# Two gate products of a recurrent branch, split by heads into 64-row matmuls

## The chip, the cores and the metric

The kernel runs on one core of a Trainium2 chip. The metric is device time in microseconds, as the median of several runs of one program. TensorE is called PE here, VectorE DVE, ScalarE ACT, GpSimd POOL and SyncE SP, as the profile calls them.

## The reference

A block of an encoder for one sequence of 512 tokens and 1024 channels: RMS norm, one wide projection, three token mixers side by side (a gated convolution, a gated linear recurrence RG-LRU, and RWKV-7 time mixing), a gated merge, an output projection, and a squared-ReLU MLP. What the change touches are the two gate products of RG-LRU. There are 16 heads of 64 channels, and both gates multiply each head's `u` by a 64 x 64 matrix of that head:

```
xb = x.reshape(Bsz, S, LRU_HEADS, LRU_BW)
gate_a = sigmoid(einsum('bshi,hij->bshj', xb, w_a).reshape(Bsz, S, C) + b_a)
gate_i = sigmoid(einsum('bshi,hij->bshj', xb, w_i).reshape(Bsz, S, C) + b_i)
log_a = -LRU_C * gate_a * softplus(a_param)
a = exp(log_a)
u = x * gate_i * sqrt(-expm1(2.0 * log_a))
```

A linear recurrence over time with `a` and `u` follows.

## The kernel before

All tiles hold channels on the 128 partitions and the 512 tokens along the free axis. For accuracy each fp32 operand of a large product is split into a high and a low fp32r part, and a product is three matmuls (`mm3`, lines 166 to 168: high by high, high by low, low by high) that add up in one PSUM bank. A projection (`proj`, line 307) is 8 such triples, 24 matmuls of 128 x 128 weights by 512 tokens, out of `hh` and `hl`; its weights come by DMA into `raw`, are cast to `whi` on ACT (line 145) and subtracted to `wlo` on DVE (line 102), three buffers deep. Its bank is from pool `pp`.

The recurrent branch lies in `ab(q)`, q from 0 to 7, two heads of 64 channels each. Its gate products take `u` split into `uh` and `ul`, and the gate weights from `load_sw` with the tag `swb`. Each gate's weight is a 128 x 128 tile with two 64 x 64 blocks on the diagonal (two heads) and zeros elsewhere, one tile per gate:

```
swh, swl = load_sw(wk, "swb", q, 2, 2)
pga = pm.tile([P, S], F32, tag="pm", name="pga")
mm3(pga, swh[:, 0], swl[:, 0], uh, ul)
ga = W("u2")
ac.activation(ga, pga, AF.Tanh, bias=pv("ba", q), scale=0.5)
```

and the same once more for `pgi` and `gi` (lines 776 to 784). I call the six matmuls of one q a gate set, and count the sets from 1 to 8 (q = 0 to 7). The pool `pm`, from which both banks come, has two banks, and others use it too: in `amat` (line 517) the 16 products pA of a half of the chunks go to four banks, three of pool `pc` and one of `pm`; four multiplies by a mask on DVE (`AXt`, line 529) read and free them; then 16 transposes pB (line 548) go through four such banks and are copied out by ACT (line 549). The pA products are 64 rows deep, and turn by turn in the lower and the upper half of the rows.

The order of the work comes from a scheduler that places the instructions on each engine by its own estimate of their times. `weave` (line 831) lets a critical generator (`krv`, `amat`, `inverse`, `chain`) run at a raised priority and feeds it pieces of `ab` and later `gate` as filling. So the gate sets stand between other work: set 1 beside `amat` of group 0, set 2 beside group 1, set 4 beside group 2, sets 3, 5, 6 and 7 among projections, and set 8 within `chain`, the steps over 8 chunks of RWKV-7 (pu, py, pS: small matmuls of 64 columns). Each engine works through its instructions in the order given. ACT after a gate computes `a`, `ga` and a GELU (lines 787 to 798).

`gate(q)` (line 735) loads another 128 x 128 weight from the same array `sw` (index 4 of 5), and `pack` (line 1051) lays these arrays out on the host.

Of the kernel before, what the change touches and what calls it, by code (L numbers as in the profile page):

```python
# [9 lines left out]
F32 = mybir.dt.float32  # L10
# [8 lines left out]
P = 128  # L19
# [77 lines left out]
def block_kernel(ctx, tc, xt, win, par, mulr, sw, wout, w1, w2, fg, cst, eyes, out):  # L97
# [67 lines left out]
    def mm3(ps, wh, wl, xh, xl, start=True, stop=True):  # L165
        pe.matmul(ps, wh, xh, start=start, stop=False)  # L166
        pe.matmul(ps, wh, xl, start=False, stop=False)  # L167
        pe.matmul(ps, wl, xh, start=False, stop=stop)  # L168
# [566 lines left out]
    def gate(q):  # L735

        yc = wk.tile([P, S], F32, tag="g3", name="yc")
        gp.dma_start(yc, mpd[q])
        gt = wk.tile([P, S], F32, tag="gc", name="gc")
        t = yield from proj(("gc", q))  # L740
        ac.activation(gt, t, AF.Tanh, bias=pv("mgc", q), scale=0.5)
        swh, swl = load_sw(wk, "swc", q, 4, 1)
        pg = pm.tile([P, S], F32, tag="pm", name="pg2")
        mm3(pg, swh[:, 0], swl[:, 0], lgh, lgl)
        stt(gt, gt, 1.0, pg, ADD, MUL)
        GQ[q] = gq_tile(q)
        ac.activation(GQ[q], gt, AF.Copy, scale=dvp(HLG, q))
        stt(gt, BV[q], pv("lb", q), gt, ADD, MUL)
        stt(BV[q], gt, 0.5, yc, MUL, ADD)
        yield  # L750

    def ab(q):
# [20 lines left out]
        t = yield from proj(("c", q))  # L773
        ac.copy(cs, t)
        yield
        swh, swl = load_sw(wk, "swb", q, 2, 2)
        pga = pm.tile([P, S], F32, tag="pm", name="pga")
        mm3(pga, swh[:, 0], swl[:, 0], uh, ul)
        ga = W("u2")
        ac.activation(ga, pga, AF.Tanh, bias=pv("ba", q), scale=0.5)  # L780
        pgi = pm.tile([P, S], F32, tag="pm", name="pgi")
        mm3(pgi, swh[:, 1], swl[:, 1], uh, ul)
        gi = W("u3")
        ac.activation(gi, pgi, AF.Tanh, bias=pv("bi", q), scale=0.5)
        stt(u, gi, 1.0, u, ADD, MUL)
        a = W("u4")
        ac.activation(a, ga, AF.Exp, scale=dvp(N4, q), bias=dvp(N4, q))
# [263 lines left out]
def pack(inp):  # L1051
    g = {k: np.ascontiguousarray(np.asarray(a)) for k, a in inp.items()}
    z = {}
    z["xt"] = g["x"].reshape(S, D).T.reshape(KT, P, S)
    win = g["w_in"][0]
    cols = np.concatenate(COLS)
    z["win"] = win[:, cols].reshape(KT, P, len(COLS), P).transpose(2, 1, 0, 3).reshape(len(COLS), P, 1024)
    nat = lambda a: a.reshape(KT, P).T
    per = lambda a: a[PERM].reshape(KT, P).T
    mu = g["rwkv_mu"][0]  # L1060
    vecs = {"mu_k": mu[1024:2048], "mu_r": mu[0:1024], "kk": g["rwkv_kk"][0], "ka": g["rwkv_ka"][0],
            "w0": g["rwkv_w0"][0], "a0": g["rwkv_a0"][0], "rk": g["rwkv_rk"][0].reshape(-1),
            "mu_v": mu[2048:3072], "ap": g["lru_a_param"][0], "lcb": g["lru_conv_b"][0],
            "ba": g["lru_ba"][0], "bi": g["lru_bi"][0], "lg": g["rwkv_lnx_g"][0],
            "lb": g["rwkv_lnx_b"][0], "mga": g["merge_b"][0][0:1024],
            "mgb": g["merge_b"][0][1024:2048], "mgc": g["merge_b"][0][2048:3072],
            "n1": g["norm1_g"][0], "n2": g["norm2_g"][0]}
    for i in range(3):
        vecs[f"ca{i}"] = g["conv_a_w"][0, i]
    for i in range(4):  # L1070
        vecs[f"lc{i}"] = g["lru_conv_w"][0, i]
    z["par"] = np.stack([(per if n in PAR_Q else nat)(vecs[n]) for n in PAR], axis=1)
    z["mulr"] = mu[3072:3328].reshape(2, P).T
    sw = np.zeros((8, P, 5, P), np.float32)
    g2 = g["rwkv_g2"][0][:, PERM]
    for j in range(8):
        js = slice(j * P, (j + 1) * P)
        sw[j, 0:64, 0] = g["rwkv_w2"][0][:, js]
        sw[j, 64:128, 0] = g["rwkv_w2"][0][:, js]
        sw[j, 0:64, 1] = g["rwkv_a2"][0][:, js]  # L1080
        sw[j, 64:128, 1] = g["rwkv_a2"][0][:, js]
        sw[j, :, 4] = g2[:, js]
        for jj in range(2):
            hd = PERM[j * P + 64 * jj] // 64
            r = slice(64 * jj, 64 * jj + 64)
            sw[j, r, 2, r] = g["lru_wa"][0, hd]
            sw[j, r, 3, r] = g["lru_wi"][0, hd]
    z["sw"] = sw
    z["wout"] = g["w_out"][0][PERM].reshape(KT, P, KT, P).transpose(2, 1, 0, 3).reshape(KT, P, 1024)
    z["w1"] = g["mlp_w1"][0].reshape(KT, P, NF, P).transpose(2, 1, 0, 3).reshape(NF, P, 1024)  # L1090
    z["w2"] = g["mlp_w2"][0].reshape(NF, P, 1024)
    z["fg"] = g["final_g"].reshape(1, D)
    cst = np.zeros((P, 3, P), np.float32)
    idx = np.arange(P)
    cst[:, 0] = np.eye(P)
    cst[:, 1] = (idx[:, None] // 64) == (idx[None] // 64)
    s_, t_ = idx[:, None] % 64, idx[None] % 64
    cst[:, 2] = np.where(idx[None] < 64, s_ < t_, s_ <= t_)
    z["cst"] = cst.reshape(P, 3 * P)
    z["eyes"] = np.tile(np.eye(32, dtype=np.float32).reshape(1, 1024), (P, 1))  # L1100
    return {k: np.ascontiguousarray(a, dtype=a.dtype) for k, a in z.items()}
# [21 lines left out]
```

## Time and profile before

| | |
|---|---|
| median of 3 runs | 1045.11 us (1043.26 to 1046.57) |
| the profiled execution, its own time | 1047.99 us |
| its span, first to last instruction | 1045.8 us |
| mean granted TensorE clock | 0.994 |
| busy: PE / DVE / ACT / POOL | 1023.8 / 647.1 / 479.7 / 111.0 us |
| the gate activations (lines 780 and 784), 16 in all | 5.6 + 5.6 us |

How to read it: the profile is one execution, taken instruction by instruction; 2.2 us of its own time lie outside the span. An engine's busy time is the time in which at least one of its instructions ran. A record of a matmul is longer than the distance to the next one, since a matmul's end overlaps the beginning of the next; so what a matmul costs in a stream is read from the starts. The timeline merges neighbours of the same line into one row with their count. An fp32 matmul of pA, pu or py leaves two records, an fp32r one (projections, gates) leaves one.

### The profile page before, as it was taken

The page shows a single profiled execution, that of the slowest core. Times are in us where ns is not written, and L with a number is a line of the kernel's source. Part 1 is how long each engine was busy: PE and PEld are TensorE (multiplying, and loading weights), DVE is VectorE, ACT ScalarE, POOL GpSimd, SP SyncE. Part 2 cuts the span into 40 slices and gives each one's busy share as a digit, 9 for nine tenths or more (in the row PEclk, how much of TensorE's full clock was granted, in tenths as well). Part 3 has the DMA queues.
Part 4 walks back from the last instruction along what each step waited for, and adds up shares of the span by engine and source line. Part 5 has one row for each costly group of instructions (what it writes and reads, how often), then busy time and mean ns, then how long its engine had stood idle before and what let it go on. Part 6 is the DMA issues. An engine that isn't in the chain of part 4 may idle for free.

```text
span 1045.8 us, 15536 instructions
## 1 busy us (share of the span) xinstructions
PE 1023.8 (98%) x6204; PEld 833.4 (80%) x6204; DVE 647.1 (62%) x1086; ACT 479.7 (46%) x694; POOL 111.0 (11%) x181
## 2 busy tenths in 40 slices
PE   8999999999999999999999999999999999999996
PEld 5777877888878788888788878878888888888885
DVE  6997597599865875995567787554444442222224
ACT  7756453655545636455454444343434332221124
POOL 1013011201112112012122101010000000000001
PEclk8999999999999999999999999999999999999998
DMA  7344644734446346333987424443233335333322
GB/s 227 118 128 117 176 131 128 209 111 134 121 136 176 117 140 202 113 119 115 315 263 223 160 89 153 140 161 96 89 98 101 101 99 186 98 101 101 98 84 81
DMA packets 44504, 145.23 MB, mean 139 GB/s; under 512 B 6096, under 2 KB 9680, under 8 KB 43408
## 3 DMA queue, kind: packets, MB, share of 16 engines
q1 hardware_dynamic: 29472, 91.02, 27.5%
q0 software_dynamic: 14240, 52.18, 17.3%
q8 instruction: 48, 0.79, 0.3%
q10 hardware_dynamic: 720, 1.05, 0.3%
q14 instruction: 24, 0.20, 0.1%
HBM read 117.49 MB, written 26.74 MB: 138 GB/s over the span
## 4 chain that ended last, share of the span: by engine, by line
PE 86%; DVE 10%; issue 2%; ACT 1%; DMA 1%; SPq 0%; DVEq 0%; ACTq 0%
PE pp L166 13%; PE pp L167 13%; PE pp L168 13%; PE acc L166 7%; PE acc L167 7%; PE acc L168 7%; PE p L167 5%; PE p L166 5%; PE p L168 5%; DVE wlo L102 2%; PE py L662 1%; PE pu L652 1%; PE pu L672 1%; DVE rk L105 1%; PE pB L548 1%
## 5 line engine op out<-in xcount | busy, mean ns | idle before, releaser
L102 DVE TENSOR_TENSOR wlo<-raw,whi 128x1024 fp32r<-128x1024 f32 (+1 forms) x164 | 198.0, 1208 | 262.7 <-ACT whi L145 262.7
L145 ACT CAST whi<-raw 128x1024 fp32r<-128x1024 f32 (+1 forms) x164 | 169.9, 1036 | 323.1 <-PE acc L168 125.0
L166 PE MATMUL pp<-hh,whi 128*128 128x512 f32 x688 | 271.0, 394 | 0.4 <-DVE rs L105 0.4
L167 PE MATMUL pp<-hl,whi 128*128 128x512 f32 x688 | 270.1, 393 | 0.0
L168 PE MATMUL pp<-hh,wlo 128*128 128x512 f32 x688 | 269.1, 391 | 0.2 <-DVE wlo L102 0.2
L166 PEld LDWEIGHTS pp<-hh,whi 128*128 128x128 f32 x688 | 129.1, 188 | 28.6 <-DVE rs L105 0.9
L168 PEld LDWEIGHTS pp<-hh,wlo 128*128 128x128 f32 x688 | 129.2, 188 | 27.6 <-DVE wlo L102 0.6
L167 PEld LDWEIGHTS pp<-hl,whi 128*128 128x128 f32 x688 | 129.2, 188 | 26.4
L166 PE MATMUL p<-h2h,whi 128*128 128x512 f32 (+1 forms) x264 | 101.4, 384 | 0.0
L167 PE MATMUL p<-h2l,whi 128*128 128x512 f32 (+1 forms) x264 | 101.2, 383 | 0.0
L168 PE MATMUL p<-h2h,wlo 128*128 128x512 f32 (+1 forms) x264 | 101.1, 383 | 0.0
L166 PE MATMUL acc<-whi,ah 128*128 128x512 f32 x256 | 99.6, 389 | 0.0
L167 PE MATMUL acc<-wlo,ah 128*128 128x512 f32 x256 | 99.6, 389 | 0.0
L168 PE MATMUL acc<-whi,al 128*128 128x512 f32 x256 | 99.6, 389 | 0.0
L168 PEld LDWEIGHTS p<-h2h,wlo 128*128 128x128 f32 x264 | 49.6, 188 | 9.7
L166 PEld LDWEIGHTS p<-h2h,whi 128*128 128x128 f32 x264 | 49.6, 188 | 9.7
L167 PEld LDWEIGHTS p<-h2l,whi 128*128 128x128 f32 x264 | 49.7, 188 | 9.5
L168 PEld LDWEIGHTS acc<-whi,al 128*128 128x128 f32 x256 | 48.0, 188 | 10.1
L166 PEld LDWEIGHTS acc<-whi,ah 128*128 128x128 f32 x256 | 48.0, 188 | 9.9
L167 PEld LDWEIGHTS acc<-wlo,ah 128*128 128x128 f32 x256 | 48.0, 188 | 9.9
L992 ACT CAST ah<-r 128x512 fp32r<-128x512 f32 x32 | 19.9, 622 | 43.4 <-DVE r L102 43.4
L102 DVE TENSOR_TENSOR al<-r,ah 128x512 fp32r<-128x512 f32 x32 | 22.2, 692 | 21.5 <-ACT ah L992 21.4
(308 smaller groups left out, 1344.9 us busy)
## 6 DMA issues: line engine op xcount, KB each, us to landing
raw<-in_win SPq DMA_DIRECT2D x88, 512.0 KB, 3.7
raw<-in_w SPq DMA_DIRECT2D x64, 512.0 KB, 3.5
ax<-axd POOLq DMA_DIRECT2D x8, 1024.0 KB, 9.5
axd<-AXt POOLq DMA_DIRECT2D x12, 512.0 KB, 7.3
bkd<-BKT POOLq DMA_DIRECT2D x4, 1024.0 KB, 13.7
raw<-in_wout SPq DMA_DIRECT2D x8, 512.0 KB, 3.5
bk<-bkd POOLq DMA_DIRECT2D x7, 512.0 KB, 12.2
swr<-in_sw SPq DMA_DIRECT2D x16, 128.0 KB, 3.0
```

Source lines behind the costliest of these rows:

```text
L102: return v.tensor_tensor(out=o, in0=a, in1=b, op=op)
L105: return v.scalar_tensor_tensor(out=o, in0=a, scalar=s, in1=b, op0=op0, op1=op1)
L145: ac.copy(hi[:, sl], raw[:, sl])
L166: pe.matmul(ps, wh, xh, start=start, stop=False)
L167: pe.matmul(ps, wh, xl, start=False, stop=False)
L168: pe.matmul(ps, wl, xh, start=False, stop=stop)
L548: pin(c2 + i, lambda: pe.transpose(pt[:, i], G_.BK[:, jj, c].rearrange("p a t -> p (a t)"), ident))
L652: pin(n, lambda: pe.matmul(pu[64 * h:64 * h + 64, x], ax[rows, g, 0, e], sv[rows, g, e], start=True, stop=True))
L662: pin(behind, lambda: pe.matmul(py[64 * h:64 * h + 64, x], w, y, start=first and x == 0, stop=last, skip_group_check=True))
L672: pin(n, lambda: pe.matmul(pu[64 * h:64 * h + 64, x], tc_[:, g, e], u0[:, g, e], start=True, stop=True))
L992: ac.copy(ahi, r)
```

## The change

The gate weights of one q are packed into one 128 x 128 tile. Its rows 0 to 63 belong to the first head and hold the 64 columns of gate a and then the 64 of gate i; its rows 64 to 127 belong to the second head and hold gate i and then gate a. A product is taken for each half of the rows by itself: 64 rows by 128 columns by 512 tokens, three matmuls each, into two banks. The first bank then holds the first head's gate a in its lower partitions and its gate i in the upper ones; the second bank has the second head's, the other way round. So the matmuls stay six per q, but each is 64 rows deep, and they are issued turn by turn, first half, second half. The two activations of 128 partitions become four of 64; gate i is written from one half of the partitions into the other, and its bias is rolled by 64 to match. `load_sw` loads 128 columns instead of 256. Both banks are allocated together.

```
-        swh, swl = load_sw(wk, "swc", q, 4, 1)
+        swh, swl = load_sw(wk, "swc", q, 3, 1)
...
-        swh, swl = load_sw(wk, "swb", q, 2, 2)
-        pga = pm.tile([P, S], F32, tag="pm", name="pga")
-        mm3(pga, swh[:, 0], swl[:, 0], uh, ul)
-        ga = W("u2")
-        ac.activation(ga, pga, AF.Tanh, bias=pv("ba", q), scale=0.5)
-        pgi = pm.tile([P, S], F32, tag="pm", name="pgi")
-        mm3(pgi, swh[:, 1], swl[:, 1], uh, ul)
-        gi = W("u3")
-        ac.activation(gi, pgi, AF.Tanh, bias=pv("bi", q), scale=0.5)
+
+        swh, swl = load_sw(wk, "swb", q, 2, 1)
+        pgs = [pm.tile([P, S], F32, tag="pm", name="pga") for _ in range(2)]
+        lo, hi = slice(0, 64), slice(64, 128)
+        for i, (w, x) in enumerate(((swh, uh), (swh, ul), (swl, uh))):
+            for pg, r in zip(pgs, (lo, hi)):
+                pe.matmul(pg, w[r, 0], x[r], start=i == 0, stop=i == 2)
+        ga, gi = W("u2"), W("u3")
+        for pg, r, o in zip(pgs, (lo, hi), (hi, lo)):
+            ac.activation(ga[r], pg[r], AF.Tanh, bias=part[r, PI["ba"], q:q + 1], scale=0.5)
+            ac.activation(gi[r], pg[o], AF.Tanh, bias=part[o, PI["bi"], q:q + 1], scale=0.5)
...
+    z["par"][:, PI["bi"]] = np.roll(z["par"][:, PI["bi"]], 64, axis=0)
...
-    sw = np.zeros((8, P, 5, P), np.float32)
+    sw = np.zeros((8, P, 4, P), np.float32)
...
-            sw[j, r, 3, r] = g["lru_wi"][0, hd]
+            sw[j, r, 2, 64 - 64 * jj:128 - 64 * jj] = g["lru_wi"][0, hd]
```

The scheduler builds the order anew. The total of PE's matmuls stays the same. Three places show what becomes of it; A and B stand for the first and the second half of the rows.

PE at set 3, among projections (pp), before:

```order
L167 MATMUL pp<-hl,whi 128x512
L168 MATMUL pp<-hh,wlo 128x512
L166 MATMUL pga<-uh,swbh 128x512
L167 MATMUL pga<-ul,swbh 128x512
L168 MATMUL pga<-uh,swbl 128x512
L166 MATMUL pgi<-uh,swbh 128x512
L167 MATMUL pgi<-ul,swbh 128x512
L168 MATMUL pgi<-uh,swbl 128x512
L166 MATMUL pp<-hh,whi 128x512
```

and now:

```order
L167 MATMUL pp<-hl,whi 128x512
L168 MATMUL pp<-hh,wlo 128x512
L782 MATMUL pga<-uh,swbh 128x512 x2
L782 MATMUL pga<-ul,swbh 128x512 x2
L782 MATMUL pga<-uh,swbl 128x512 x2
L166 MATMUL pp<-hh,whi 128x512
L167 MATMUL pp<-hl,whi 128x512
```

Each row "x2" is a pair, A and then B, into the two banks. The same turn by turn order stands in sets 1, 6, 7 and 8; in set 5 it is A A B B A B.

PE behind set 1, from the first pA burst towards the pB transposes, before:

```order
L526 MATMUL pA<-AR,BK 128x128 x16
L166 MATMUL pp<-hh,whi 128x512
L167 MATMUL pp<-hl,whi 128x512
L168 MATMUL pp<-hh,wlo 128x512
L166 MATMUL pp<-hh,whi 128x512
L167 MATMUL pp<-hl,whi 128x512
L168 MATMUL pp<-hh,wlo 128x512
L526 MATMUL pA<-AR,BK 128x128 x16
L166 MATMUL pp<-hh,whi 128x512
L167 MATMUL pp<-hl,whi 128x512
L168 MATMUL pp<-hh,wlo 128x512
L166 MATMUL pp<-hh,whi 128x512
```

and now, from the second piece of pA on (a lone pA and nine projection matmuls stand ahead of it, directly behind the gates):

```order
L526 MATMUL pA<-AR,BK 128x128 x15
L166 MATMUL pp<-hh,whi 128x512
L526 MATMUL pA<-AR,BK 128x128 x2
L167 MATMUL pp<-hl,whi 128x512
L526 MATMUL pA<-AR,BK 128x128
L168 MATMUL pp<-hh,wlo 128x512
L166 MATMUL pp<-hh,whi 128x512
L526 MATMUL pA<-AR,BK 128x128 x13
L167 MATMUL pp<-hl,whi 128x512
L168 MATMUL pp<-hh,wlo 128x512
L166 MATMUL pp<-hh,whi 128x512
L167 MATMUL pp<-hl,whi 128x512
```

The two pA bursts of 16 are cut into five pieces with projection matmuls between them. Between the gates and pB stood 10 projection matmuls; now 17 do.

PE at set 2, before:

```order
L526 MATMUL pA<-AR,BK 128x128 x16
L166 MATMUL pga<-uh,swbh 128x512
L167 MATMUL pga<-ul,swbh 128x512
L168 MATMUL pga<-uh,swbl 128x512
L166 MATMUL pp<-hh,whi 128x512
L548 MATMUL pB<-ident,BK 128x128 x12
L166 MATMUL pgi<-uh,swbh 128x512
L548 MATMUL pB<-ident,BK 128x128 x4
L167 MATMUL pgi<-ul,swbh 128x512
L168 MATMUL pgi<-uh,swbl 128x512
L167 MATMUL pp<-hl,whi 128x512
```

and now:

```order
L526 MATMUL pA<-AR,BK 128x128 x16
L782 MATMUL pga<-uh,swbh 128x512
L782 MATMUL pga<-ul,swbh 128x512
L782 MATMUL pga<-uh,swbl 128x512
L166 MATMUL pp<-hh,whi 128x512
L548 MATMUL pB<-ident,BK 128x128 x12
L782 MATMUL pga<-uh,swbh 128x512
L548 MATMUL pB<-ident,BK 128x128 x4
L782 MATMUL pga<-ul,swbh 128x512
L782 MATMUL pga<-uh,swbl 128x512
L167 MATMUL pp<-hl,whi 128x512
```

The places are the same: three A, then, apart from them, three B. Set 4 is like it: three A right behind a pA burst, six projection matmuls, three B right ahead of the next pA burst (before, the second gate's three stood there too, with four projection matmuls between). Behind set 8 one group of 16 pu matmuls, cut into 1 and 15 before, stands in one piece.

On ACT the four activations of a set stand together, but for set 1, where a cast `whi` stands behind the first of them, and set 2, where the four copies behind pB stand between the A and the B ones. On DVE behind set 4 the product of the GELU (line 792 before, `u3<-u3,g2`), which stood ahead of the four AXt multiplies, stands behind them; the product with gate i (line 785 before) stays ahead.

## Rows read from the trace of the kernel before

**Rows 1.** Page, parts 1 and 4: PE's busy time, and the chain that ended last, by engine.
```profile
PE 1023.8 (98%) x6204; PEld 833.4 (80%) x6204; DVE 647.1 (62%) x1086; ACT 479.7 (46%) x694; POOL 111.0 (11%) x181
...
PE 86%; DVE 10%; issue 2%; ACT 1%; DMA 1%; SPq 0%; DVEq 0%; ACTq 0%
```

**Rows 2.** Timeline of PE, third gate set: start us, us, engine, line, op, out<-in.
```profile
222.05 0.39 PE L166 MATMUL pga<-uh,swbh 128*128 128x512 f32 x1
...
223.43 0.39 PE L166 MATMUL pp<-hh,whi 128*128 128x512 f32 x1
```

**Rows 3.** Timeline of PE at the start of a pA burst.
```profile
178.20 0.38 PE L526 MATMUL pA<-AR,BK 64*128 64x128 f32 x2
```

**Rows 4.** By tile, pA and the gate activation: ns min/median/max, first and last start.
```profile
L526 PE MATMUL pA<-AR,BK x256: 272/272/373, 89.3 to 392.7; 64*128 64x128 f32 x128
...
L780 ACT ACTIVATE u<-pga,part x8: 687/692/732, 88.7 to 539.6; 128x512 f32<-128x512 f32 x8
```

**Rows 5.** Timeline of PE around the second pA burst of group 1.
```profile
177.87 0.40 PE L168 MATMUL pp<-hh,wlo 128*128 128x512 f32 x1
178.20 2.06 PE L526 MATMUL pA<-AR,BK 64*128 64x128 f32 x32
180.18 0.50 PE L166 MATMUL pga<-uh,swbh 128*128 128x512 f32 x1
180.52 0.39 PE L167 MATMUL pga<-ul,swbh 128*128 128x512 f32 x1
```

**Rows 6.** Timeline of all engines behind the fourth gate set.
```profile
306.41 2.48 DVE L102 TENSOR_TENSOR AXt<-pA,mask 128x512 f32<-128x512 f32 x4
...
311.83 0.69 DVE L102 TENSOR_TENSOR u<-u,g 128x512 f32<-128x512 f32 x1 [1.36 <-ACT u L791]
...
312.44 2.48 DVE L102 TENSOR_TENSOR AXt<-pA,mask 128x512 f32<-128x512 f32 x4
...
313.78 1.97 PE L548 MATMUL pB<-ident,BK 128*128 128x128 f32 x16 [1.13 <-DVE AXt L102]
```

**Rows 7.** Timeline of PE: one chain matmul between projections.
```profile
551.92 0.39 PE L167 MATMUL pp<-hl,whi 128*128 128x512 f32 x1
552.24 0.33 PE L652 MATMUL pu<-sv,ax 128*64 128x64 f32 x2
...
552.84 0.39 PE L166 MATMUL pp<-hh,whi 128*128 128x512 f32 x1
```

**Rows 8.** Timeline of PE behind the eighth gate set.
```profile
539.37 0.40 PE L168 MATMUL pgi<-uh,swbl 128*128 128x512 f32 x1
539.70 1.15 PE L652 MATMUL pu<-sv,ax 128*64 128x64 f32 x32
```

**Rows 9.** Timeline of all engines behind the first gate set.
```profile
87.81 0.40 PE L166 MATMUL pga<-uh,swbh 128*128 128x512 f32 x1
...
92.39 2.48 DVE L102 TENSOR_TENSOR AXt<-pA,mask 128x512 f32<-128x512 f32 x4
...
93.13 3.02 PE L526 MATMUL pA<-AR,BK 64*128 64x128 f32 x32
...
96.08 0.50 PE L166 MATMUL pp<-hh,whi 128*128 128x512 f32 x1
...
98.11 1.97 PE L548 MATMUL pB<-ident,BK 128*128 128x128 f32 x16 [0.84 <-DVE AXt L102]
```

**Rows 10.** Groups of ACT, 86 to 500 us: busy us, mean ns, idle before and releasers.
```profile
L145 ACT CAST whi<-raw 128x1024 fp32r<-128x1024 f32 x64 | 67.0, 1047 | 94.6 <-PE pp L167 62.3 <-DMA raw<-in_win 21.4 <-issue 9.8
```

**Rows 11.** Two ACT copies by line, 64 rows and 128 rows deep.
```profile
L656 ACT COPY u<-pu x8: 582/584/587, 504.7 to 596.3; 64x512 f32<-64x512 f32 x8
...
L774 ACT COPY g<-pp x8: 576/580/622, 88.0 to 539.1; 128x512 f32<-128x512 f32 x8
```

**Rows 12.** Waits of PE: us in total, times, longest.
```profile
PE pB L548 <- DVE AXt L102: 2.3, 3, 1.1
...
PE pp L168 <- DVE wlo L102: 0.2, 1, 0.2
```

More of the change, by code (lines that the diff above doesn't have):

```diff
@@ L1081, in pack @@
         sw[j, 64:128, 1] = g["rwkv_a2"][0][:, js]
-        sw[j, :, 4] = g2[:, js]
+        sw[j, :, 3] = g2[:, js]
         for jj in range(2):
```

## The prediction

> **What bounds the kernel now.** I read the page first. PE is busy for 1023.8 of 1045.8 us, and the chain of work that ended last is 86% PE [rows 1]. So a time on PE's own stream counts in full, and a time on another engine counts only where PE waits for it. Next the timeline of PE around the third gate set. Its first matmul starts at 222.05 and the first projection matmul behind its six at 223.43, so a 128-row matmul of 512 columns takes (223.43 - 222.05) / 6 = 0.23 us in the stream [rows 2], although its own record is longer (0.39 us, since neighbours overlap). I call 0.23 us a slot. The eight sets are 48 slots, 11.0 us in all. That is the whole sum that can be played for.
>
> **The slots that overlap.** The change makes each of the 48 matmuls 64 rows deep, and lets a pair in different row halves stand side by side. The trace has such pairs: the pA matmuls alternate between the halves. The first two records of a burst end 0.38 us after the first began, and one takes 0.27 at least, so they ran beside each other [rows 3, 4]. In the steady part 32 records of pA take 2.06 us, while 16 records of pB, as wide but 128 rows deep, take 1.97 us [rows 5, 6]. So a pair of halves costs what one full record costs. pA has 128 columns in plain fp32, the gates 512 in fp32r; I take the same overlap.
>
> Only neighbours in the order overlap, and the two halves' order is not the same in every set. In sets 1, 3, 6, 7 and 8 the halves alternate: three overlaps each. In set 5 the order is A A B B A B, where the second A overlaps the first B and the second B the third A: two. In sets 2 and 4 three A stand together and the B come later: none. That makes 17 slots, 17 x 0.23 = 3.9 us, and not 24.
>
> **The crossings.** Between 128-row and 64-row work PE does not flow on. Into the pA burst, the next start comes 178.20 - 177.87 = 0.33 us after the last projection matmul, 0.10 over a slot. Then the first weight load lies open: the first pair needs 0.38 us, where the median record takes 0.27 [rows 3, 4]. Out of it the first full matmul takes 0.50 instead of 0.39, its next start comes 0.34 after it, and it began some 0.09 late [rows 5]. So a crossing costs 0.20 us, and a trip there and back 0.40. The shortest trip in the trace bounds it: one chain matmul (pu, two records) sits between two projection matmuls, and from the one ahead of it (551.92) to the second one behind it (552.84) 0.92 us pass instead of two slots, 0.46 [rows 7]. Taking off 0.06 to 0.11 for the matmul itself leaves 0.35 to 0.40. This is the term that works against the change. The Trainium skill, TensorEngine Tiling (Array Packing), Key Properties, says that a change of the tiling mode, not of the tile alone, drains TensorE. By that rule the trace agrees, with the start 0.10 us late; the page has no price for it.
>
> **The sum on PE, set by set.**
> - Sets 3, 6, 7 stand between projections: 3 x 0.23 - 0.40 = 0.29 saved each, 0.87.
> - Set 5: 2 x 0.23 - 0.40 = 0.06 saved.
> - Set 8 is followed directly by a chain matmul, whose crossing existed already (539.37 to 539.70, 0.33 us [rows 8]). Only one crossing is new: 0.69 - 0.20 = 0.49 saved.
> - Set 2: the three A follow pA and cross nothing more. The B are cut apart by the pB transposes, one and then two, so two trips are new: 0.80 lost, nothing saved.
> - Set 4: the A follow one pA burst, the B stand ahead of the next. The number of trips stays: 0.
> - Behind set 8 the scheduler no longer cuts one pu matmul off its group of 16. That trip [rows 7] goes: 0.40 saved.
>
> Together 0.87 + 0.06 + 0.49 + 0.40 - 0.80 = 1.0 us saved.
>
> **Set 1 and the waits behind it.** Here the order changes most: pA is cut into 1, 15, 2, 1 and 13, five stays in 64-row mode instead of two. Counted bare that is three trips more (1.2 us) and, as four of the pieces are odd, two more slots of a pA pair (two records each, 2 x 0.22), against 0.69 saved by the gates. But PE waits there in the trace. The second pA burst takes 3.02 us instead of 2.06, because each bank is freed by one of the four AXt multiplies on DVE, which run from 92.39 for 2.48 us; and pB idles 0.84 us for the next AXt [rows 9]. The cuts fill these waits with projection matmuls: 17 stand between the gates and pB instead of 10. I walk it from 87.81. Crossing, gates and a lone pA to 88.9; nine projections to 91.2; then the bank that two gate activations free, with a weight cast (1.05 us [rows 10]) between them: 91.4 (88.9 when the gates stop, + 0.69 + 1.05 + 0.69). Fifteen pA to 93.5 with the last one's end. The AXt begin there, and as before the second burst ends 3.7 us after they begin (92.39 to 96.08): 97.2. pB follows 2.0 us later, as before: 99.2 instead of 98.11. That is 1.1 us later with seven slots (1.6 us) more done: 0.5 saved. Bounds: 1.2 saved if every cut falls into a wait, and 1.0 lost if none does.
>
> **Set 4 and the waits behind it.** pB waits 1.13 us for AXt, and AXt began only at 312.44, because ahead of it on DVE stood a product that waited 1.36 us for ACT [rows 6]. In the new order that product stands behind AXt; only the product with the input gate is ahead. It waits for the fourth gate activation: set B stops near 310.0 (it waits for AXt's release of its bank until 308.9), two activations of 0.69 to 311.4, the product to 312.1. AXt starts 0.3 earlier: 0.3 saved, between 0.6 and -0.8 (if the bank comes 1 us later).
>
> **What ACT, DVE and the queues get.** Two activations of 0.69 us become four [rows 4], and half the rows do not halve the time: an ACT copy of 64 rows takes 0.584, one of 128 rows 0.580 [rows 11]. That is 2 x 0.69 = 1.4 us per set, 11 us in all, less what a smaller cast of the gate weights saves. I cost it at nothing: PE waited 0.2 us in total for weight splits [rows 12], and ACT itself idles 94.6 us ahead of 64 weight casts between 86 and 500 us, mostly for PE to free a buffer [rows 10]. If that cover went, each set would pay up to 1.4 us. Queued behind the added activations are a weight cast, the gate chain and, in sets 1, 2 and 4, the copies that follow pB. Both pm banks are now held at once, until two and four activations are through; who waits for them is pA and pB, costed above. DVE's subtraction and SP's DMA for these weights halve; nothing waits for either.
>
> **The forecast.** 1.0 + 0.5 + 0.3 = 1.8 us less. The profiled execution took 1047.99 us with a span of 1045.8; on it the sum gives 1046.2 and a span of 1044.0. The median of the three runs is 1045.11, 2.9 under the profiled one, and the same sum gives **1043.3**. That is 0.17% faster. About 0.3% (3.1 us, so 1042.0 and 1048.2) is what a measurement of this kernel can tell from no change: I forecast a gain too small to see.
>
> **Rivals.**
> - *Crossings cost nothing with 512 columns* (the next weights load under the long stream). Then the 17 overlaps count in full: 1045.1 - 3.9 = 1041.2. For it: the gate streams are four times as long as pA's, so a load has more to hide under. Against it: the late start of pA came behind a 512-column matmul. Chance 0.20. The Trainium skill, TensorEngine Tiling (Array Packing), Theoretical Speedup, gives up to 2x where a dimension is at most 64; by that alone half of the 48 slots, 5.5 us, would go, and the time would be 1039.6, but the order holds no 24 overlaps.
> - *ACT becomes the wait, and the kernel is slower.* The three waits for pB (2.3 us in total [rows 12]) lie right behind sets 1, 2 and 4. If each grows by the two added activations, 3 x 1.38 = 4.1 us come on, and the 0.8 of sets 1 and 4 do not arrive: 1045.1 - 1.0 + 4.1 = 1048.2. It decides once the added waits pass 1.0 us. For it: FIFO order on ACT with a weight cast between the activations of set 1. Against: in set 4 DVE's order takes the worst wait away. Chance 0.07.
> - *The change does not do what it says*: the halves run one after the other at 512 columns. Then 3.9 us of slots stay and the crossings are paid: 1043.3 + 3.9 = 1047.2. The pairs of [rows 3] speak against it. Chance 0.06.
>
> **Numbers.** The forecast has 0.67. Its own range, from the bounds of sets 1 and 4 and crossings of 0.35 to 0.46, with the 1.6 us by which the runs spread, is 1041.2 to 1046.0. The range takes in the first rival and leaves the other two out (0.13): 1041.0 to 1046.0. Faster by over 0.3%: the first rival and a tail of the forecast, 0.22. Slower by over 0.3%: mostly the second rival, 0.07. Within: 0.71.
>
> **What the new profile would show.** Right: gate records in pairs, 0.9 us from the first gate matmul of set 3 to the first projection behind it (0.34 and 0.23 between the pairs, 0.32 out) instead of 1.38; open weight loads (0.50 us records) behind each set; sets 2 and 4 without a gain; pB's waits in total no longer than 2.3 us. Wrong: pairs that start a slot apart; no longer records behind the sets; pB or pA waiting for the gate activations by over 1 us.

## The result and the profile after

| | before | changed |
|---|---|---|
| median of 20 runs each | 1044.14 us (1043.26 to 1047.21) | 1047.62 us (1044.26 to 1050.21) |
| ratio | | 1.0023, 95% interval 1.0014 to 1.0032 |
| profiled execution, its own time and span | 1047.99 and 1045.8 us | 1046.41 and 1044.6 us |

The change makes the kernel slower by 0.23%, some 2.4 us, where 0.17% faster was forecast. (The two medians alone lie 3.5 us apart; I go by the ratio and its interval. The forecast had started from the median of three runs, 1.0 us above that of twenty.) The page of the changed kernel, parts 1 and 4 [rows 1]:

```profile
PE 1022.1 (98%) x6204; PEld 828.8 (79%) x6204; DVE 646.4 (62%) x1086; ACT 491.3 (47%) x710; POOL 111.0 (11%) x181
...
PE 82%; DVE 11%; ACT 3%; DMA 2%; issue 2%; SPq 0%; DVEq 0%; ACTq 0%
```

PE is busy 1.7 us less. But ACT is busy 11.6 us more, as the forecast had it, and ACT and the DMAs have 5% of the chain where they had 2%. In the list of PE's waits (us in total, times, longest) the ones for `sv` and `u` are new, the one at pn had 1.2 us before, and the one at pB had 2.3 [rows 12]:

```profile
PE pn L452 <- ACT a L443: 2.0, 2, 1.3
PE pS L681 <- ACT sv L674: 1.9, 1, 1.9
...
PE pu L672 <- ACT u L656: 0.9, 1, 0.9
PE pB L548 <- DVE AXt L102: 0.9, 2, 0.6
...
PE pA L526 <- ACT u L786: 0.5, 1, 0.5
```

The products themselves do what was forecast. The timeline of PE at set 3 [rows 2]:

```profile
221.76 0.49 PE L782 MATMUL pga<-uh,swbh 64*128 64x512 f32 x2
222.09 0.39 PE L782 MATMUL pga<-ul,swbh 64*128 64x512 f32 x2
222.32 0.40 PE L782 MATMUL pga<-uh,swbl 64*128 64x512 f32 x2
222.65 0.50 PE L166 MATMUL pp<-hh,whi 128*128 128x512 f32 x1
```

Each row is a pair in the time of one; the pairs start 0.33 and 0.23 apart, the first projection stands 0.89 us behind the first gate matmul, and its record has 0.50.

The table says where most of the 2.4 us come from. Each stretch runs from the first gate matmul of one set to that of the next (or to a chain step), read from PE's timeline; "pu0" and "pu7" are the first and the eighth group of 16 pu products from `sv`, one group in each of the 8 chunks (a second pu group of a chunk is from `u`). A row's forecast is that of the set that begins it; a plus is time saved. A row ends with the way into the next set, so where only that one is new, as from set 2 to 3, 0.1 us of it belongs to the next set.

| stretch | before | changed | gained | forecast |
|---|---|---|---|---|
| set 1 to 2 | 92.37 | 92.86 | -0.5 | +0.5 |
| set 2 to 3 | 41.87 | 42.85 | -1.0 | -0.8 |
| set 3 to 4 | 84.20 | 83.65 | +0.55 | +0.29 |
| set 4 to 5 | 90.16 | 89.65 | +0.5 | +0.3 |
| set 5 to 6 | 39.49 | 39.63 | -0.15 | +0.06 |
| set 6 to 7 | 41.85 | 41.56 | +0.3 | +0.29 |
| set 7 to pu0 | 23.91 | 23.54 | +0.4 | +0.29 |
| **pu0 to set 8** | 35.48 | 37.31 | **-1.8** | 0 |
| set 8 to pu7 | 56.12 | 56.13 | 0 | +0.89 |

(For set 7 to pu0 a second trace of before is taken; the first holds a 1.0 us wait there, ahead of pu0.) The sum is -1.7 us, within the interval; read from the second trace of either kernel it is -1.2, and set 1 to 2 takes 92.71 and 92.57 us there, so that row is within what two executions differ by.

Two things lie outside the table. One is the granted clock of TensorE: its mean over an execution is 0.9959 in the 20 executions of the changed kernel and 0.9960 in 11 more, while 29 of the kernel before, run beside those 11, have 0.9971, and its other series 0.9966 to 0.9969. With PE busy 98% of the span that is 0.7 to 1.2 us of the 2.4, an estimate from these shares; the last section shows such a fall of the clock. The other is a wait in the part of the program that was not touched, `tp` for ACT near 690 us: 0.3 to 0.6 us in some executions and 1.8 to 2.6 in others. It is long in five of six traces with the full change, and in one of four of the kernel before and its controls. That is too few to say whether the change makes it long more often; a part of the 2.4 us may lie there.

### The profile page after: what moved, and what is told of

Its sections match the earlier page's. It is cut to its first block, busy times and chain, and to the rows that moved or that the text cites. A ratio compares the mean times of both kernels' runs of the same rounds, so it can differ in the third digit from the quotient of the medians.

```text
span 1044.6 us, 15561 instructions
## 1 busy us (share of the span) xinstructions
PE 1022.1 (98%) x6204; PEld 828.8 (79%) x6204; DVE 646.4 (62%) x1086; ACT 491.3 (47%) x710; POOL 111.0 (11%) x181
## 4 chain that ended last, share of the span: by engine, by line
PE 82%; DVE 11%; ACT 3%; DMA 2%; issue 2%; SPq 0%; DVEq 0%; ACTq 0%
PE pp L167 12%; PE pp L166 12%; PE pp L168 12%; PE acc L168 7%; PE acc L167 7%; PE acc L166 7%; PE p L166 5%; PE p L168 5%; PE p L167 5%; DVE wlo L102 2%; DMA raw<-in_win 1%; PE py L662 1%; ACT whi L145 1%; DVE rk L105 1%; PE pB L548 1%
```

## Experiments

**The halves of the change apart.** Copies of both kernels ran beside two kernels with one half each.

> The kernel before once more, for a second profile. All theories: same time within 0.1%. In the first profile a pu matmul waits 1.0 us near 502 us and pB 2.3 us in three waits; a theory that these waits hang on the phase of the DMAs expects them to differ here by 0.5 us or more, a theory that they come from the order alone expects them equal within 0.1 us.

> The changed kernel once more, for a second profile and times on the same chip as the parts. All theories: 2 to 3 us slower than before. In its first profile PE waits 1.9 us for ACT ahead of pS near 506 us (behind a weight cast whose DMA landed late), 0.9 us ahead of pu near 542 us and 0.8 us ahead of pn near 125 us: if these are the loss, they stand here too, with 2 us or more in total.

`act4_old_matmuls` keeps the 128-row products and only splits each activation:

```
-        ac.activation(ga, pga, AF.Tanh, bias=pv("ba", q), scale=0.5)
+        for r in (slice(0, 64), slice(64, 128)):
+            ac.activation(ga[r], pga[r], AF.Tanh, bias=part[r, PI["ba"], q:q + 1], scale=0.5)
```

> The old 128-row products, but each gate activation cut into two of 64 partitions (four per set, 1.4 us of ACT more per set). If ACT and the order that the scheduler makes of it cost the time (the matmuls being worth some 1 us of gain): slower than before by 2 to 4 us, with the waits near 506 and 542 us. If the crossings between 64-row and 128-row work are the loss: same as before within 0.7 us.

`mm64_act2` has the paired products with one activation of 128 partitions per bank:

```
-        for pg, r, o in zip(pgs, (lo, hi), (hi, lo)):
-            ac.activation(ga[r], pg[r], AF.Tanh, bias=part[r, PI["ba"], q:q + 1], scale=0.5)
-            ac.activation(gi[r], pg[o], AF.Tanh, bias=part[o, PI["bi"], q:q + 1], scale=0.5)
+        ac.activation(ga, pgs[0], AF.Tanh, bias=pv("ba", q), scale=0.5)
+        ac.activation(gi, pgs[1], AF.Tanh, bias=pv("bi", q), scale=0.5)
```

> The 64-row products in pairs, but one activation of 128 partitions on each bank, two per set as before; the output mixes the two gates, so part of the computation is changed. The order of PE then is that of before but for the turns of the halves. If ACT is the loss: faster than before by 0.5 to 1.5 us (sets 3, 5, 6, 7 and 8 gain 1.4, sets 1 and 2 lose 0.8 at most). If the crossings are the loss: slower than before by 1.5 to 3 us.

Measured ratios: before again 0.9999 [0.9991, 1.0008], changed again 1.0019 [1.0007, 1.0032], four activations alone 1.0025 [1.0014, 1.0035], paired products alone 1.0020 [1.0010, 1.0030]. So the activations alone cost all that the change costs, and the products alone do not win but lose as much: the halves do not add up, and `mm64_act2` came out as expected if the crossings were the loss, not ACT. Its crossings are no dearer than forecast, though (0.40 us for the trip at set 3, as in the changed kernel), and the traces tell more. With the activations split, pu0 to set 8 takes 38.0 us, and in the paired products with two activations 35.2: the largest loss belongs to the activations. Set 1 to 2 takes 93.31 with the activations split, so they cost 0.6 to 0.9 us there too. The paired products pay in set 2 (42.85) and set 4 (90.72). Their set 1 (93.26) is no measure, since in that execution the clock was granted at 0.50 for 3.4 us from 93.1, behind a wait of 0.9 us at pA. Over its 11 executions the mean clock of `mm64_act2` is 0.9955, the lowest of these four; against 0.9971 that is some 1.7 of its 2.1 us, by the same estimate. Why its clock falls more often is not shown.

**Why PE waits at pS.** The timeline of all engines of the changed kernel, from the weight cast behind set 7 to the state product of chunk 0:

```profile
486.43 1.03 ACT L145 CAST whi<-raw 128x1024 fp32r<-128x1024 f32 x1
...
487.48 1.28 ACT L800 ACT_TABLE_LOAD   x1
487.49 1.23 DVE L102 TENSOR_TENSOR wlo<-raw,whi 128x1024 fp32r<-128x1024 f32 x1 [0.25 <-ACT whi L145]
488.75 0.33 SPq L134 DMA_DIRECT2D raw<-in_win  x1
...
490.77 1.22 DVE L804 TENSOR_TENSOR_SCAN u<-u,u 128x512 f32<-128x512 f32 x1
...
495.33 0.33 SPq L134 DMA_DIRECT2D raw<-in_win  x1
...
506.40 1.04 ACT L145 CAST whi<-raw 128x1024 fp32r<-128x1024 f32 x1 [4.07 <-DMA raw<-in_win]
...
507.35 0.58 ACT L674 COPY sv<-pu 64x512 f32<-64x512 f32 x1
...
507.98 1.15 PE L681 MATMUL pS<-sv,bk 128*64 128x64 f32 x32 [1.88 <-ACT sv L674]
```

and the same stretch of the kernel before:

```profile
486.70 1.28 ACT L798 ACT_TABLE_LOAD   x1
...
488.53 1.03 ACT L145 CAST whi<-raw 128x1024 fp32r<-128x1024 f32 x1
...
489.51 1.22 DVE L802 TENSOR_TENSOR_SCAN u<-u,u 128x512 f32<-128x512 f32 x1
...
490.65 1.20 DVE L102 TENSOR_TENSOR wlo<-raw,whi 128x1024 fp32r<-128x1024 f32 x1
...
491.88 0.33 SPq L134 DMA_DIRECT2D raw<-in_win  x1
...
496.55 0.33 SPq L134 DMA_DIRECT2D raw<-in_win  x1
...
507.25 1.05 ACT L145 CAST whi<-raw 128x1024 fp32r<-128x1024 f32 x1 [1.97 <-PE pp L167]
...
508.20 0.58 ACT L674 COPY sv<-pu 64x512 f32<-64x512 f32 x1
...
509.00 1.15 PE L681 MATMUL pS<-sv,bk 128*64 128x64 f32 x32
```

Read from the end. pS waits for the copy `sv`, which stands on ACT behind a weight cast, and this cast waits 4.07 us for its row `raw`, issued at 495.33 (call it Y). Before, the cast does not wait for the DMA. At the start of the stretch the order has turned: with two activations more in set 7, the scheduler put a weight cast ahead of the square root's table load and its split on DVE ahead of the scan. The split frees a buffer, and another row (X) is issued at 488.75, 1.9 us ahead of the first load of the chain's chunks (`sv`, 490.69); before, X went out with that load (491.88 and 491.76).

My first theory was that bk of chunk 1, issued ahead of Y in the changed kernel and behind it before, delays Y.

```
-        if c < NC - 1:
+        if c < NC - 1 and c != 1:
             gp.dma_start(flat(bk), flat(bkd[c]))
...
+            if c == 0:
+                gp.tensor_copy(nxt[4][0:1, 0, 0:1], u0[0:1, 0, 0, 0:1])
+                gp.dma_start(nxt[4].rearrange("p x t -> p (x t)"), bkd[1].rearrange("p g e t -> p (g e t)"))
```

> Control: the kernel before, with one DMA held back. The state weights bk of chunk 1 (512 KB) are started only when u0 of chunk 0 exists (a one-element copy on POOL makes the DMA wait for it), so that the weight row raw of the projections does not land behind them. No other instruction moves on any engine. In the two traces of before the first state product pS waits for nothing, so no theory expects a gain: from the first pu to the second group of pu 9.85 us as before, ratio 1.000 (0.999 to 1.001). If holding bk back has a price of its own (the state product of chunk 1 then waits for bk), the stretch from pu1 to pu2 grows beyond its 11.4 to 12.0 us.

> The changed kernel with the same DMA held back, nothing else moved. Theory A (the added activations move a weight split on DVE ahead of the scan, the next raw starts 2 us sooner, sv of chunk 0 lands sooner, and so bk of chunk 1 is issued at 495.2 to 496.5, ahead of the third raw, instead of 497.3 to 499.4; raw lands at 506.3 to 508.4 instead of 504.9 to 506.0; the cast of whi on ACT waits for it, the copy sv stands behind the cast, and PE waits 1.9 to 2.6 us at pS): the wait at pS goes, the stretch from pu0 to pu1 falls from 11.8-12.6 to 9.8-9.9 us, the time falls by about 2.0 to 1044.4, ratio to before 1.000 (0.999 to 1.001). Theory B (ACT is simply too full in this stretch, the bk transfer has nothing to do with it): the cast stays late, the stretch keeps 11.8 to 12.6, ratio 1.002. Theory C (the transfer only moves its cost): the pS wait goes but a wait for bk of up to 2 us comes in chunk 1, ratio 1.001 to 1.002.

The control came out at 0.9995 [0.9981, 1.0009], the changed kernel at 1.0021 [1.0007, 1.0034]: nothing won. The timeline of `after_bk_held` shows Y late without bk in its way:

```profile
507.26 1.04 ACT L145 CAST whi<-raw 128x1024 fp32r<-128x1024 f32 x1 [4.56 <-DMA raw<-in_win]
```

That theory fell. The next run takes the copy off ACT's queue:

```
-            ac.copy(sv[0:64, :, 2:4], by_tile(pu[64:128]))
+            (v.tensor_copy if c == 0 else ac.copy)(sv[0:64, :, 2:4], by_tile(pu[64:128]))
```

> The changed kernel with the second half of the sv copy of chunk 0 (64x512) on DVE behind the first half instead of on ACT, so that it no longer stands behind the cast of whi that waits for raw; raw itself lands as late as before. Theory A (it is the place in ACT's queue that makes PE wait at pS): the wait of 1.9 to 2.1 us falls to the price of a second copy on DVE, 0.6 to 0.7 us less the overlap, so 0 to 0.4; the stretch from pu0 to pu1 falls to 9.9 to 10.3 us; time 1044.4 to 1044.9, ratio 1.000 (0.999 to 1.002). Rival (the projections behind pS need the same late whi): PE then waits 1.5 to 2 us at the first projection on it instead, and nothing is won: ratio 1.002.

It gave 1.0027 [1.0012, 1.0042]. The wait at pS is gone, but ACT is as late as before, and the next product waits for ACT's next copy; from the list of waits of `after_sv_on_dve`:

```profile
PE pu L652 <- ACT sv L649: 1.5, 1, 1.5
```

So the late cast is the cause of the wait, whichever copy stands behind it. Next to this, with bk still held, I asked for the six products of a set in one piece, with the call `pin` that the chain uses (line 171):

```
-            for pg, r in zip(pgs, (lo, hi)):
-                pe.matmul(pg, w[r, 0], x[r], start=i == 0, stop=i == 2)
+            for k, (pg, r) in enumerate(((pgs[1], hi), (pgs[0], lo))):
+                pin(i + k, lambda: pe.matmul(pg, w[r, 0], x[r], start=i == 0, stop=i == 2))
```

> The changed kernel with bk held back and the six gate products of a set asked for next to each other: the first where it is free to go, on the other bank, and the five behind it in one piece, alternating between the halves. In sets 2, 4 and 5, where the scheduler had put two runs of three or an uneven turn, two overlaps come in place of none (sets 2 and 4) and the runs are one trip. Expected by the slot of 0.23, the crossing of 0.20 and the trip of 0.40 us: set 2 loses 0.3 instead of the measured 0.98 (0.6 better), set 4 gains 0.3, set 5 0.1 to 0.2; with the 2.0 of the pS wait together 3.0 under the changed kernel: 1043.4, ratio to before 0.999 (0.998 to 1.000). If overlap is not what decides in set 2 (its loss is a wait for a bank instead), its stretch from g2 to g3 keeps 42.86 us and the ratio is 1.000.

1.0013 [1.0000, 1.0027], where 0.999 was expected. 1.7 us of the wait at pS stayed. Set 2 to 3 fell by 0.3 us instead of 0.6, set 4 to 5 did not move, and set 5 to 6 grew by 0.2. The first product still stood alone, a trip of its own, with the second bank not yet free.

**The early row.** Now X itself is held back, by a copy from the product ahead of the scan (`C["u"]`, kept behind `tt(u, u, ga, MUL)`), and the paired products are put into a few sets only (`if q in PAIRED`; the others keep the old code and weights).

```
+            C["n"] = C.get("n", 0) + 1
+            if C["n"] == 76:
+                v.tensor_copy(w[0][0:1, 0:1], C["u"][0:1, 0:1])
             sy.dma_start(w[0], src)
```

> The changed kernel with one weight row held back by some 2 us: the raw that was issued at 488.7 to 489.5 (right behind the weight split which the added activations let DVE take ahead of the scan) waits for a one-element DVE copy that itself waits for the product in front of the scan, so it is issued at about 491.5 to 492, together with the chunk loads, as in the kernel before. Nothing else moves on any engine. Theory A2 (it is this early row that lets the chunk loads start 1.2 us sooner, so that the raw after next, issued near 496, has 2.36 to 2.4 MB of them in front of it instead of 1.9 to 2.0, lands at 507 instead of 505, and holds the cast whi, the copy sv behind it, and PE): the raw issued near 496 lands by 506, the wait at pS falls from 1.9-2.4 to under 0.7 us, the stretch from pu0 to pu1 from 11.8-13.8 to 9.8-10.6, the ratio to before to about 1.0005 (0.999 to 1.002). Theory B (ACT is late there for its own fullness): the stretch stays at 11.8 or more.

> The kernel before with the paired 64-row products and their four activations in the third and the sixth set alone; PE's order is that of before but for the turns of the halves, POOL's is the same, and on DVE the weight split stays behind the scan. The PE terms (slot 0.23, crossing 0.20) and the trace of the changed kernel give 0.37 to 0.38 us for each set at its products and 0.1 behind the third: 0.8 to 0.9 us in all, ratio 0.9992 (0.998 to 1.000). The stretch from pu0 to pu1 stays 9.85 us. If the added activations cost something by themselves wherever they stand, the gain is eaten: ratio 1.0000 or more.

> The same with the seventh set paired as well. PE gains another 0.37 us there, and PE's and POOL's orders stay those of before; but the two added activations of this set make DVE take the weight split ahead of the scan, as in the changed kernel. Theory A2: the early row and its consequence come with it, the stretch from pu0 to pu1 grows from 9.85 to 11.8-12.6 us and the kernel ends 1.6 us or more behind pairs_3_6: ratio 1.0007 (0.999 to 1.002). Theory B (fullness of ACT from all eight sets): no wait at pS, 0.37 us better than pairs_3_6, ratio 0.9988.

> Sets 3, 6 and 7 paired, and the early raw held back as in after_raw_held (on DVE the one-element copy, and one weight split that changes places with a neighbour, are the only differences to pairs_3_6_7). Theory A2: pu0 to pu1 is back at 9.8 to 10.6 us, and the three sets' 1.2 us are left: ratio 0.9989 (0.998 to 1.0005). If holding the row back does not help: as pairs_3_6_7.

| kernel | median us | ratio | pu0 to set 8 |
|---|---|---|---|
| after_raw_held | 1046.46 | 1.0013 [1.0000, 1.0025] | 37.0 |
| pairs_3_6 | 1043.66 | 0.9982 [0.9970, 0.9995] | (below) |
| pairs_3_6_7 | 1046.01 | 1.0010 [0.9998, 1.0022] | 37.8 |
| pairs_3_6_7_raw_held | 1042.50 | 0.9976 [0.9965, 0.9987] | 35.1 |

Pairing set 7 as well costs 2.3 us in the medians though PE saves 0.29 more at its products, both crossings counted; holding X back gives 3.5 back, 2.7 of it in the stretch from pu0 to set 8. In `pairs_3_6_7` X is issued at 488.40, ahead of the loads, and its list of waits has

```profile
PE pS L682 <- ACT sv L675: 2.4, 1, 2.4
```

while with X held no wait for ACT is left there. The timeline of `pairs_3_6_7_raw_held`:

```profile
490.21 0.13 DVE L139 COPY raw<-u 1x1 f32<-1x1 f32 x1
...
490.41 15.88 SPq L140 DMA_DIRECT2D raw<-in_win  x4
...
503.62 1.05 ACT L151 CAST whi<-raw 128x1024 fp32r<-128x1024 f32 x1 [1.97 <-PE pp L173]
...
504.58 0.57 ACT L680 COPY sv<-pu 64x512 f32<-64x512 f32 x1
...
505.35 1.15 PE L687 MATMUL pS<-sv,bk 128*64 128x64 f32 x32
```

The cast waits for PE again, as before the change. In the full change (`after_raw_held`) the same edit won only 0.3 to 0.5 us of the stretch: 1.6 us of wait for `sv` stay. Why it helps less there is open.

**What was still open.**

> Control for pairs_3_6_7_raw_held: the kernel before with the same row held back by the same one-element DVE copy (here it is issued some 0.8 us later than before, behind the start of the chunk loads instead of with it), nothing else moved. PE does not wait at pS in before, so holding the row back wins nothing: ratio 1.0000 (0.999 to 1.001), pu0 to pu1 9.85 us. Rival (the held row is what made pairs_3_6_7_raw_held fast, through the later transfers): ratio 0.998 to 0.9985.

> The same kernel as pairs_3_6_7_raw_held, for a second set of runs. The checkpoints of its first trace give 1.2 us on PE between the first gate product and the first MLP product, that is 0.9988; the first runs gave 0.9976 [0.9965, 0.9987]. Expected 0.9982 (0.997 to 0.999).

> The kernel before with the first set alone paired, four activations there. Forecast for this set was 0.5 us saved. In the changed kernel the products won 0.65 us (from g1 to pA1 1.46 to 0.81), but the stretch behind them to pB0 took 1.5 to 1.9 us more, and the one from there to the second set 1.0 less: the order of PE behind the set is another (the pA products of the next tiles stand later) and PE waits 0.3 and 0.4 us at pA for the activation u. Theory: the four activations, 0.68 us each one behind the other, hold the banks that the pA products need, so that the whole stretch from g1 to the second set takes 92.4 to 92.9 us as in before (92.4 to 92.7): no gain, ratio 1.000 (0.999 to 1.001). If the loss in the changed kernel came from the second set's code instead, this run has g1 to the second set at 91.9 to 92.2.

> The kernel before with the eighth set alone paired. Forecast 0.5 saved at its products and 0.4 at the pu product no longer cut off. Theory: the products win 0.59 us (g8 to pu3 0.89 instead of 1.48), then PE waits 0.9 us at pu for the copy u that stands behind the four activations on ACT, and the stretch from g8 to the seventh pu group is as long as before (54.6 to 56.1): ratio 1.000 (0.999 to 1.001). pu0 to pu1 stays at 9.85 since the seventh set is unchanged. Rival (the loss there came from the late weights of pS in front of it): no wait at pu, 0.6 to 0.9 us faster, ratio 0.9992.

The control missed, and usefully: 1.0045 [1.0030, 1.0060]. In the kernel before, the same copy stands behind one more instruction on DVE, X goes out 0.7 us behind the first load (492.20 and 491.47) instead of 0.1, and comes so late that the cast for X waits; from the timeline of `before_raw_held`:

```profile
500.69 1.05 ACT L150 CAST whi<-raw 128x1024 fp32r<-128x1024 f32 x1 [5.77 <-DMA raw<-in_win]
...
505.86 0.58 ACT L661 COPY u<-pu 64x512 f32<-64x512 f32 x1 [2.12 <-issue]
...
506.49 1.15 PE L677 MATMUL pu<-u,tc 64*64 64x64 f32 x32 [2.23 <-ACT u L661]
```

So holding a row back is no gain by itself. The best kernel repeats: 0.9980 [0.9970, 0.9990], 1042.70 us; from set 1 to the MLP its two traces take 593.2 and 593.1 us, where `before_again` and `before_bk_held`, with little or no wait ahead of pu0, take 594.7 and 594.4. Of these 1.2 to 1.6 us the pairs of sets 3, 6 and 7 are 0.9, 0.29 each; most of the remainder lies between pu0 and set 8 (35.1 against 35.3 to 35.7). A part of the rest of the 2.1 to 2.5 us can be the wait ahead of pu0 for the load `ax`. In the five traces that have this wait, 0.2 to 1.5 us (1.0 in the first one of before), set 7 is unchanged and pu0 starts 0.3 to 0.4 us behind the landing of `ax`; in the two of the best kernel `ax` has landed 1.4 and 2.0 us ahead of pu0. How much that is on average was not measured.

The first set alone gives 1.0005 [0.9994, 1.0017]; set 1 to 2 takes 92.68 us. PE wins 0.65 us at the products and one of the waits for pB, and gives both back. From the list of waits of `pairs_1`:

```profile
PE pn L453 <- ACT a L444: 1.9, 2, 1.2
...
PE pB L549 <- DVE AXt L103: 1.5, 2, 1.2
```

The first of the two waits for pn, 0.7 us, is new, and pA waits 0.5 us; the remainder is left to PE's order, whose cut pA the forecast had priced at three trips, 1.2 us. The eighth set alone gives 1.0011 [0.9999, 1.0023]; set 8 to pu7 takes 56.15 us, as before. Its timeline shows the gain eaten one step on:

```profile
537.76 0.68 ACT L786 ACTIVATE u<-pga,part 64x512 f32<-64x512 f32 x1
...
538.45 0.68 ACT L787 ACTIVATE u<-pga,part 64x512 f32<-64x512 f32 x1
...
539.16 0.69 ACT L786 ACTIVATE u<-pga,part 64x512 f32<-64x512 f32 x1
...
539.87 0.68 ACT L787 ACTIVATE u<-pga,part 64x512 f32<-64x512 f32 x1
...
540.58 0.81 ACT L800 ACTIVATE u<-u,dv 128x512 f32<-128x512 f32 x1
...
541.42 0.58 ACT L657 COPY u<-pu 64x512 f32<-64x512 f32 x1
...
542.05 1.15 PE L673 MATMUL pu<-u,tc 64*64 64x64 f32 x32 [0.91 <-ACT u L657]
```

Four activations of 0.68 us stand where two of 0.69 did [rows 4], the copy `u` goes out behind them, and PE waits 0.91 us for it. But the two added activations are not the whole reason. In the kernel before, the copy had nothing to spare: it ended at 544.11, and the product on it started at 544.16.

```profile
543.52 0.59 ACT L656 COPY u<-pu 64x512 f32<-64x512 f32 x1
...
544.16 1.15 PE L672 MATMUL pu<-u,tc 64*64 64x64 f32 x32
```

And `mm64_act2`, with the pairs and two activations, waits at the same product and takes 56.06 us from set 8 to pu7. From its list of waits:

```profile
PE pu L672 <- ACT u L656: 0.5, 1, 0.5
```

So what PE saves at the eighth set's products is waited away at this copy with two activations too.

## Why the prediction was wrong

- **The slot, the overlap and the crossing were right.** From the last projection matmul ahead of set 3, 6 or 7 to the second one behind it 1.84 us passed, and now 1.54 to 1.55: 0.29 saved each, as forecast. That the halves run at the same time only as neighbours was right too: in sets 2 and 4 no A and B start together.
- **Set 2 was sized about right**: -0.9 for -0.8, as 0.1 of its row is the way into set 3. The timeline of PE there:

```profile
182.03 0.50 PE L782 MATMUL pga<-uh,swbh 64*128 64x512 f32 x1
182.46 0.66 PE L548 MATMUL pB<-ident,BK 128*128 128x128 f32 x4
183.05 0.50 PE L782 MATMUL pga<-ul,swbh 64*128 64x512 f32 x1
183.38 0.39 PE L782 MATMUL pga<-uh,swbl 64*128 64x512 f32 x1
183.71 0.50 PE L167 MATMUL pp<-hl,whi 128*128 128x512 f32 x1
```

  Out of the lone B the next start comes 0.43 us after it, out of the pair of B 0.33 after the last: both crossings cost, twice. The Trainium skill, TensorEngine Tiling (Array Packing), Key Properties, has TensorE drain at a change of the mode. By that rule the trace agrees: this set, with two trips and no pair, loses 0.9 us.
- **Set 4 was right** (+0.5 for +0.3), by the reason given: DVE's order let the second AXt begin 5.58 us behind the set's first matmul instead of 6.19, and the wait for pB there fell from 1.13 to 0.57 us. This order comes with the split activations: they alone win as much (`act4_old_matmuls`, 89.68), while the pairs alone lose 0.6 (`mm64_act2`).
- **Set 5 was off by 0.2**: the two overlaps did not pay for the trip and the uneven turns.
- **The step that failed is "I cost it at nothing"**, of ACT's added 11 us. I had looked for waits for weight splits, and for ACT's idle time between 86 and 500 us. What ACT hands to PE there in time is not all: it also copies between the steps of the chain, from 500 us on, and stands in front of DVE's product in the gate chain. Three things came of it. Set 7's added activations reorder a weight split, move the row X by 2 us, and end in 1.9 us of waiting at pS, the largest term of all. In set 1 they and the new order cost what the overlap wins; the share of each is not separated. And in set 8 PE waits 0.9 us for the copy `u`, which eats the 0.89 forecast there and at the pu product no longer cut off. There a second step failed with it, "a time on PE's own stream counts in full": the copy was only just in time before, and 0.5 us of waiting came even with two activations. I had also read the order of ACT and DVE around sets 1, 2 and 4 only, and not behind set 7, where it turned. The lower granted clock, by estimate 0.7 to 1.2 us, had no term in the sum at all.
- **The signs were too narrow.** The pairs, the 0.89 us at set 3, the records of 0.50 and pB's waits came as the forecast had named them for being right, and the kernel was slower: none of these signs looked at what ACT hands over in the chain.
- **The rival "ACT becomes the wait"** had the right engine and sign, at 0.07, but the wrong place: it put the waits at pB, which became shorter. It should have had a price for each place at which PE waits for anything on ACT.

That the added activations of set 7 bring the wait at pS is shown by `pairs_3_6`, `pairs_3_6_7` and the held row, and by the halves: the activations alone have 2.6 us of it, the pairs alone none. How the transfers of X, Y and the chunk loads share the queues, so that both an earlier and a later X make a row late, is not settled.

## What to carry to other kernels

An engine that is idle half of the time is no cover by that: list each place where the bounding engine waits for it, or receives from it with little to spare, and price the added instructions there. Where a scheduler rebuilds the order, compare the order of the feeding engines and queues behind every copy of the changed piece, not only beside those where PE's order moves. And try a change piece by piece: of eight equal sets three, with one row held back, were worth 0.2%, while all eight cost as much.

## What the runs showed of the hardware that I had not expected

With the start of one 512 KB row against the chunk loads go some 2 us. Where it was issued 1.9 to 2.1 us ahead of the first load, in the changed kernel and five others with four activations in set 7, PE waited 1.5 to 2.6 us for ACT in the first two chunks. Issued within 0.5 us of that load, there was no such wait in nine of ten traces (1.6 us in `after_raw_held`); issued 0.7 us behind it, 2.2 us.

In the trace of `pairs_3_6` PE waited 1.47 us ahead of the first pu group, and was then granted 0.55 and 0.53 of its clock, near the lower of its two levels (1.2 of 2.4 GHz), for some 4 us (columns: window, its length, each engine's busy us, PEclk, DMA share, GB/s):

```profile
500.90:502.00 1.10, 1.10 (x33) 1.03 (x33) 0.00 (x0) 0.00 (x0) 0.55 (x1) 1.00 1.09 291
502.00:505.00 3.00, 3.00 (x9) 1.94 (x7) 0.68 (x1) 0.59 (x1) 0.00 (x0) 0.53 1.00 298
```

That is why its stretch from pu0 is not in the table. In the profiled execution of the changed kernel the clock stayed at 1.00 behind the wait of 1.88 us at pS, but in that of `after_bk_held` it fell to the lower level behind the wait of 2.37 us there:

```profile
510.20:513.60 3.40, 3.40 (x31) 2.89 (x27) 3.00 (x5) 1.48 (x4) 1.62 (x3) 0.50 0.80 293
```

The trace of `pairs_8` has such a fall too, 3.4 us from 691.5, behind the 2.2 us at `tp`. So in some executions a fall of the clock comes on top of a wait of PE, in others not, and a single trace does not show how often.
